# A two-layer decoder trunk on one core: the order of all five engines written out, with the convolution and the second compression in one tiled block

## The chip, the core and the metric

The kernel runs on one core of one Trainium2 chip (trn2). The metric is device time in microseconds (us) of one execution, median over runs; the profile is of one more execution. The engines are TensorE (PE: matmuls, with PEld its weight loads), VectorE (DVE), ScalarE (ACT), GpSimd (POOL) and SyncE (SP, which here only issues loads).

## The reference, cut to what matters

```python
def hybrid_layer(x, ...):                       # x: (1, 256, 1024), two layers
    h = rms_norm(x, norm_g)
    z = h @ w_in                                # 3612 columns, split among three groups of heads
    o_a = fox_attention(q, k, v, f_logit) * silu(f_gate)         # 4 heads x 64, forget gates
    o_b = conformer_conv(glu_in, ...) * silu(c_gate)             # 31 causal taps on 256 channels
    o_c = nsa_attention(q, kc, vc, ks, vs, kw, vw, ...) * silu(n_gate)
    return x + concat(o_a, o_b, o_c) @ w_out
# in nsa_attention (8 query heads in 2 groups g):
def compress(x, pe, w1, w2):                    # blocks of 32 tokens, stride 16: 15 blocks
    blk = x[:, cmp_idx] + pe                    # -> (15 blocks, 2 groups, 32 * 64)
    return gelu(blk @ w1) @ w2                  # w1: 2048 x 256, w2: 256 x 64
k_cmp = rope(compress(kc, pe_k, k_w1, k_w2), cmp_end)
v_cmp = compress(vc, pe_v, v_w1, v_w2)
# branches: softmax over compressed blocks, over selected blocks, over a window; mixed by gates
```

A final norm follows the second layer. All of it is fp32.

## The kernel before

**Products in halves.** An fp32 weight tile comes by DMA in raw form (512 KB for 1024 columns); ACT copies it to a "hi" half (L240), DVE subtracts to get the "lo" half (L244), and PE then makes three products, hi by hi, hi by lo, lo by hi. The input projection's columns are cut in 24 blocks of 128, S0 to S23 (`wS`), each 24 matmuls (`s(i)`, L457 to L459), two blocks to a PSUM tile named after the even one: `ps0` is S0 and S1 (the raw keys and values to compress), `ps8` S8 and S9 (the first half of the queries), `ps10` S10 and S11 (the second half), and so on. Blocks of the output projection are O0 to O7. The matrices w1 of the two compressions are not cut in halves: eight raw tiles of 512 KB a layer, `ww1_i_q` for compression i, quarter q.

**The work around the change, in each layer.** `blocks` (L781) adds the position terms to the raw keys and values and writes `xp0` and `xp1`. `compress(i)` (L791) is 16 matmuls on a quarter of PE's columns each, four to a row of the order (`32x256 x4`), into `ph0` or `ph1`; in the trace each shows as two records. `fox_pv` (L730) is the forgetting attention's product with its values into `ofx`, 8 matmuls on half of PE's columns. `conv` (L546) is the convolution, 64 matmuls on a quarter of the columns into `pcn`, with taps `cw` that `taps` builds on DVE (L535 of the before). `hidden` (L808) brings the sums of the compressions into `hidT`, and `compressed_kv` (L830, L833) makes the compressed keys and values `pkv` from them with `w2`. `query(i)` turns and splits `ps8` or `ps10` into `qs0` and `qs1` (L474 to L477 and L761 on DVE, L760 on ACT); `scores(n)` (L859, L860) are the window's logits `sw0` to `sw7` and need `qs` and the keys `kh`, `klz`. `fpt` and `fs` are the forgetting attention's transposes and logits.

**Order.** SP, PE and POOL run in the order in which the calls are written (`manual_schedule`). DVE and ACT are placed by the scheduler, apart from the first stretch of layer 0; `mark` and `behind` only fix behind which instruction a half may be formed. `pump` issues the loads in the order of `queue` (built from `S_ORDER`), at most `RAW` = 6 raw tiles being held; a load waits until the tile six loads before it was used: a block S by its lo half, a quarter of w1 by its matmuls. `WARM` is the number of matmuls on a constant that run at the start ahead of the transposes of the norm's gain (`g0p`) and behind them (`turn`, L282).

Of the kernel before, what the change touches and what calls it, by code (L numbers as in the profile page):

```python
# [9 lines left out]
F32 = mybir.dt.float32  # L10
# [9 lines left out]
AHEAD = 4  # L20
WARM = 5, 3
LAST = 416
LAG = 1
# [38 lines left out]
W2 = {"w2k": (0, 128), "w2v": (128, 128), "pw": (256, 512)}  # L62
W2_N = 768
# [63 lines left out]
def trunk(ctx, tc, a, out, dbg=None):  # L127
    nc = tc.nc
# [8 lines left out]
    ctx.enter_context(tc.manual_schedule(engines={E.SP, E.PE, E.Pool}))  # L137
# [33 lines left out]
    S_ORDER = (2, 3, 4, 5, 12, 13, 14, 15, 6, 7, 8, 9, 0, 1, 10, 11, "w1", 16, 17, 18, 19, 20, 21, 22, 23)  # L171
    queue = []
    parts = []
    for l in range(L):
# [21 lines left out]
    marks = [{}]  # L196

    def mark():

        at = {}  # L200
        for i in reversed(nc.cur_bb.bb.instructions):
            if i.engine in (E.DVE, E.Activation) and i.engine not in at and i.name not in formed:
                at[i.engine] = i
            if len(at) == 2:
                break
        marks.append(at)

    formed = set()

    def behind(engine, made):  # L210
        at = marks[-LAG].get(engine) if len(marks) >= LAG else None
        with tc.issue_after(at) if at is not None else nullcontext():
            made()
        formed.add(nc.cur_bb.bb.instructions[-1].name)

# [17 lines left out]
    def split_hi():  # L233

        key, n = parts.pop(0)
# [4 lines left out]
        behind(E.Activation, lambda: sc.copy(hi, w))  # L240
        split[key] = hi, lo

        def low():
            behind(E.DVE, lambda: ve.tensor_tensor(lo, w, hi.bitcast(F32), op=ALU.subtract))  # L244
            used(1)
        return low

    def split_next():
        if not parts or parts[0][0] not in raws:
            return False  # L250
        split_hi()()
        return True

    def need(key, ahead=AHEAD):

        while key not in split:
            assert split_next(), key
        n = sum(1 for k in split)
        while n < ahead + 1 and split_next():
            n += 1  # L260
        return split[key]
# [137 lines left out]
    for l in range(L):  # L399
# [17 lines left out]

        def mprod(t, which, n, steps="xt", p=None):
# [18 lines left out]
            if which == "A":  # L437
                sc.copy(vsw[:, t, :], p[:, :256])
                sc.activation(gl[:, t, :], p[:, 256:280], AF.Tanh, scale=0.5)
            else:  # L440
                sc.copy(fv[:, t, :], p[:, :256])
                ve.tensor_tensor(ff[:, t, :], p[:, 256:260], S("fb"), op=ALU.add)


        bank = {}

        def s(i, ahead=AHEAD):

            mark()
            hi, lo = need(("S", i, l), ahead)  # L450
# [11 lines left out]
        def s2(i):  # L462
            return bank.pop(i // 2).rearrange("p (i t) -> p i t", i=2)
# [27 lines left out]
        def gates(i):  # L491
            p = s2(16 + 2 * i)
            u = cp.tile([128, 2, 256], F32, name=nm(f"tg{i}"), tag="tg", bufs=1)
            sc.activation(u, p, AF.Tanh, scale=0.5)
            ve.scalar_tensor_tensor(sgt[0][:, 2 * i:2 * i + 2], u, 1.0, p, op0=ALU.add, op1=ALU.mult)
# [6 lines left out]
        def mix_split(c0, n, cols=slice(0, 256)):  # L502
            m = sgt[0][:, c0:c0 + n, cols]
            h = mixh[:, c0:c0 + n, cols]
            sc.copy(h, m)
            ve.tensor_tensor(mixl[:, c0:c0 + n, cols], m, h.bitcast(F32), op=ALU.subtract)
# [9 lines left out]

        def glu(i):

            p = s2(2 + 2 * i)
            th = cp.tile([128, 512], F32, name=nm(f"th{i}"), tag="tg", bufs=1)[:, 0:256]  # L520
            sc.activation(th, p[:, 1], AF.Tanh, scale=0.5)
            ve.scalar_tensor_tensor(ypad[:, i, 30:286], th, 1.0, p[:, 0], op0=ALU.add, op1=ALU.mult)
# [8 lines left out]
        def taps(i):  # L531
            if i == 0:
                sgt[0] = cp.tile([128, 2, 32, 32], F32, name=nm("cw"), tag="sg", bufs=1)
            cw = sgt[0][:, i]
            behind(E.DVE, lambda: ve.tensor_tensor(  # L535
                cw, C("sh").unsqueeze(1).broadcast_to([128, 32, 32]),
                S("cw")[:, i * 32:(i + 1) * 32].unsqueeze(2).broadcast_to([128, 32, 32]), op=ALU.mult))
            pconv[i] = pconv[i], cw.rearrange("p (g q) c -> p g q c", g=4)

        def conv():  # L540
            p = pscore(nm("pcn"))
            for i in range(2):
                yr, w = pconv[i]
                for q in range(8):
                    for g in range(4):
                        te.matmul(p[g * 32:(g + 1) * 32, i * 256:(i + 1) * 256], w[:, g, q], yr[:, g, 4 * q:4 * q + 256],  # L546
                                  start=q == 0, stop=q == 7)
            sgt[0] = cp.tile([128, 8, 256], F32, name=nm("sg"), tag="sg", bufs=1)
            for i in range(2):
                sc.activation(yc[:, i], p[:, i * 256:(i + 1) * 256], AF.Identity, bias=S("cb")[:, i:i + 1])  # L550
# [4 lines left out]
        def ln_stats():  # L555
            pt = ln["p"] = ppt(nm("lnp"))
            st = cp.tile([128, 2, 6], F32, name=nm("st"), tag="st", bufs=1)
            mv = ln["mv"] = cp.tile([128, 2, 2], F32, name=nm("mv"), tag="mv", bufs=1)
            rv = ln["rv"] = cp.tile([128, 2], F32, name=nm("rv"), tag="rv", bufs=1)
            for t in range(2):  # L560
                for c in range(2):
                    o = t * 256 + c * 128
                    te.transpose(pt[:, o:o + 128], yc[:, c, t * 128:(t + 1) * 128], C("id"))
            for t in range(2):
# [3 lines left out]
            gp.tensor_tensor(rv, rv, mhalf[:, :2], op=ALU.pow)  # L568
            yn = ln["yn"] = cp.tile([128, 2, 256], F32, name=nm("yn"), tag="rr", bufs=2)
# [4 lines left out]
        def ln_swish():  # L574
            yn = ln["yn"]
            pn = ppt(nm("lnq"))
# [4 lines left out]
            yl = cp.tile([128, 2, 256], F32, name=nm("yl"), tag="rr", bufs=2)  # L581
# [5 lines left out]
            ve.scalar_tensor_tensor(yt, yt, 1.0, yl, op0=ALU.add, op1=ALU.mult)  # L587

        def pointwise():
# [7 lines left out]
            return pcv.rearrange("p (i t) -> p i t", i=2)  # L597
# [15 lines left out]
        def forget():  # L613
            ffv = ff.rearrange("p t h -> p (t h)")
            lsr = cp.tile([128, 512], F32R, name=nm("lsr"), tag="ru", bufs=2)
            lsh, lsl = (lsr[:, c:c + 256].rearrange("p (t h i) -> p t h i", t=2, h=4) for c in (0, 256))
            fx["ls"] = lsh, lsl
            ve.scalar_tensor_tensor(fa, ffv, -1.0, ffv, op0=ALU.mult, op1=ALU.max)
            sc.activation(fe, fa, AF.Exp, scale=-1.0)
# [631 lines left out]
```

## Time and profile before

| | us |
|---|---|
| median of 3 runs (316.72 to 316.84) | 316.83 |
| the profiled execution | 316.37 |
| its span | 314.6 |
| PE busy, of the span | 303.7 (97%) |
| DVE busy, of the span | 234.9 (75%) |
| ACT busy, of the span | 186.9 (59%) |

The span runs from the first instruction to the last; 1.77 us of the profiled execution lie outside it. Matmuls are pipelined, so the busy time of one (280 ns for 256 columns) is longer than the distance from one start to the next (about 120 ns); the distance is what counts when PE is full. A row's start is in us from the span's start.

### The profile page before, as it was taken

Reading aid. Unit: us, or ns where it says so; the run is one execution under the profiler, and the core shown is the slowest. Engines: PE = TensorE matmul, PEld = TensorE weight load, DVE = VectorE, ACT = ScalarE, POOL = GpSimd, SP = SyncE. Lnnn points to the kernel's source line nnn. Section 1 sums busy time; section 2 is a strip of 40 time slices with the busy share of each in tenths; the row PEclk is TensorE's granted clock in tenths of the full one; section 3 lists DMA queues with packets and bytes.
Section 4 is the critical chain, followed back from the end, with each engine's and each line's share of the span. In section 5 each row is a group of like instructions: output and inputs, shape, how many; then the busy total and the mean of one; then the engine's idle time right before and its main releaser. Section 6 shows DMA issues by size and latency. Waiting matters only on the chain.

```text
span 314.6 us, 6713 instructions
## 1 busy us (share of the span) xinstructions
PE 303.7 (97%) x2596; PEld 273.8 (87%) x2596; DVE 234.9 (75%) x626; ACT 186.9 (59%) x408; POOL 22.6 (7%) x49
## 2 busy tenths in 40 slices
PE   7999999999999999999999999999999999999991
PEld 5799999995789999888899999999578999988891
DVE  3957689981999998965574778998199989896532
ACT  4757668731595957861545766783259595786110
POOL 2000043000002000000000003400000200000000
PEclk9999999999999999999999999999999999999998
DMA  7797889707927445130461878880792744000101
GB/s 285 256 382 272 277 246 236 290 2 271 409 69 258 133 135 155 46 94 2 166 200 70 292 233 258 219 307 2 285 403 59 260 135 133 0 2 0 63 8 69
DMA packets 16545, 54.93 MB, mean 175 GB/s; under 512 B 2048, under 2 KB 2560, under 8 KB 16512
## 3 DMA queue, kind: packets, MB, share of 16 engines
q1 hardware_dynamic: 15264, 51.29, 46.9%
q0 software_dynamic: 960, 2.92, 4.1%
q8 instruction: 20, 0.33, 0.4%
q10 hardware_dynamic: 288, 0.28, 0.3%
q14 instruction: 13, 0.11, 0.1%
HBM read 52.85 MB, written 1.64 MB: 173 GB/s over the span
## 4 chain that ended last, share of the span: by engine, by line
PE 88%; issue 4%; DMA 4%; DVE 1%; ACT 1%; POOLq 0%; POOL 0%; DVEq 0%
PE ps L457 15%; PE ps L458 14%; PE ps L459 14%; PE pcn L546 4%; PE pA L430 4%; PE pt L915 4%; PE pB L430 4%; PE pw L982 4%; PE pw L979 4%; PE pw L978 4%; PE on L928 3%; DMA ww<-in_w 3%; PE sw L859 2%; PE sw L860 2%; DMA cf<-in_cf 1%
## 5 line engine op out<-in xcount | busy, mean ns | idle before, releaser
L457 PE MATMUL ps<-hTh,wS_1h 128*128 128x256 f32 x192 | 54.3, 283 | 0.0
L457 PE MATMUL ps<-hTh,wS_0h 128*128 128x256 f32 x192 | 54.3, 283 | 0.0
L459 PE MATMUL ps<-hTh,wS_1l 128*128 128x256 f32 x192 | 53.9, 281 | 0.0
L458 PE MATMUL ps<-hTl,wS_0h 128*128 128x256 f32 x192 | 53.9, 281 | 0.0
L459 PE MATMUL ps<-hTh,wS_0l 128*128 128x256 f32 x192 | 53.9, 281 | 0.0
L458 PE MATMUL ps<-hTl,wS_1h 128*128 128x256 f32 x192 | 53.9, 281 | 0.0
L887 ACT ACTIVATE P<-P,mx 128x128 f32<-128x128 f32 (+1 forms) x64 | 28.5, 447 | 15.1 <-DVE mx L482 15.0
L457 PEld LDWEIGHTS ps<-hTh,wS_1h 128*128 128x128 f32 x192 | 36.2, 188 | 0.6 <-issue 0.4
L457 PEld LDWEIGHTS ps<-hTh,wS_0h 128*128 128x128 f32 x192 | 36.2, 188 | 0.6 <-issue 0.4
L458 PEld LDWEIGHTS ps<-hTl,wS_1h 128*128 128x128 f32 x192 | 36.2, 188 | 0.2
L458 PEld LDWEIGHTS ps<-hTl,wS_0h 128*128 128x128 f32 x192 | 36.2, 188 | 0.2
L459 PEld LDWEIGHTS ps<-hTh,wS_1l 128*128 128x128 f32 x192 | 36.2, 188 | 0.0
L459 PEld LDWEIGHTS ps<-hTh,wS_0l 128*128 128x128 f32 x192 | 36.2, 188 | 0.0
L244 DVE TENSOR_TENSOR wS_0l<-wS,wS_0h 128x1024 fp32r<-128x1024 f32 x24 | 28.6, 1221 | 8.4 <-ACT wS_0h L240 8.4
L244 DVE TENSOR_TENSOR wS_1l<-wS,wS_1h 128x1024 fp32r<-128x1024 f32 x24 | 28.5, 1221 | 8.1 <-ACT wS_1h L240 8.1
L240 ACT CAST wS_1h<-wS 128x1024 fp32r<-128x1024 f32 x24 | 24.1, 1051 | 1.8 <-DMA wS<-in_wS 1.8
L240 ACT CAST wS_0h<-wS 128x1024 fp32r<-128x1024 f32 x24 | 24.1, 1049 | 0.5 <-DMA wS<-in_wS 0.4
L482 DVE CUSTOM_DVE_ANT_0 P<-sw,cf 128x128 f32<-128x128 f32 (+1 forms) x64 | 19.5, 355 | 2.4 <-PE sw L860 2.4
L917 ACT COPY PT<-pt 128x512 f32<-128x512 f32 x24 | 13.6, 586 | 9.6 <-PE pt L915 9.6
L985 DVE TENSOR_TENSOR x<-pw,x 128x512 f32<-128x512 f32 (+1 forms) x9 | 5.7, 631 | 16.8 <-PE pw L982 16.8
L485 DVE TENSOR_SCALAR P<-P,co 128x128 f32<-128x128 f32 (+1 forms) x64 | 16.4, 316 | 0.1
L546 PE MATMUL pcn<-yr,cw 128*32 128x256 f32 x256 | 14.2, 380 | 0.0
(239 smaller groups left out, 679.3 us busy)
## 6 DMA issues: line engine op xcount, KB each, us to landing
wS<-in_wS SPq DMA_DIRECT2D x48, 512.0 KB, 5.7
ww<-in_w SPq DMA_DIRECT2D x16, 512.0 KB, 5.3
wO<-in_wo SPq DMA_DIRECT2D x16, 512.0 KB, 4.0
yr<-ybuf POOLq DMA_DIRECT2D x16, 142.0 KB, 5.0
wA<-in_wA SPq DMA_DIRECT2D x4, 420.0 KB, 4.2
wB<-in_wB SPq DMA_DIRECT2D x4, 390.0 KB, 5.0
x<-in_x SPq DMA_DIRECT2D x2, 512.0 KB, 4.1
w<-in_w SPq DMA_DIRECT2D x2, 384.0 KB, 4.7
```

The costliest lines, as they stand in the source:

```text
L240: behind(E.Activation, lambda: sc.copy(hi, w))
L244: behind(E.DVE, lambda: ve.tensor_tensor(lo, w, hi.bitcast(F32), op=ALU.subtract))
L430: te.matmul(p[:, :n], a_[:, k, tok], b_, start=first, stop=s_ == "t" and k == 7)
L457: te.matmul(o, hi[:, k], hTh[:, k], start=k == 0, stop=False)
L458: te.matmul(o, hi[:, k], hTl[:, k], start=False, stop=False)
L459: te.matmul(o, lo[:, k], hTh[:, k], start=False, stop=k == 7)
L482: ve.tensor_tensor_reduce(o, x, m, -1.0, 3.0e38, ALU.add, ALU.min, mx)
L485: ve.tensor_scalar(x, x, r, None, op0=ALU.mult)
L546: te.matmul(p[g * 32:(g + 1) * 32, i * 256:(i + 1) * 256], w[:, g, q], yr[:, g, 4 * q:4 * q + 256], start=q == 0, stop=q == 7)
L887: sc.activation(P[:, g, b], P[:, g, b], AF.Exp, bias=mx[:, c:c + 1], scale=-1.0, accum_out=su[:, c:c + 1])
L915: te.transpose(pt[:, o + b * 128:o + (b + 1) * 128], Pg[:, b * 128:(b + 1) * 128], C("id"))
L917: sc.copy(PT, pt)
```

## The change

All five engines now run in written order: `E.DVE` and `E.Activation` join `manual_schedule`, `mark`, `behind`, `need` and `AHEAD` are gone, and the helpers are cut in steps (`form_hi` and `form_lo`, `mask` and `expo`, `query_rope` and `query`, `gate_tanh` and `gate_mul`, ...) that a long list of calls puts in order. Every formation of a half stands at a place of its own. The number of instructions is the same but for the rows below.

```diff
-WARM = 5, 3
+WARM = 8, 1
-    ctx.enter_context(tc.manual_schedule(engines={E.SP, E.PE, E.Pool}))
+    ctx.enter_context(tc.manual_schedule(engines={E.SP, E.PE, E.Pool, E.DVE, E.Activation}))
-    S_ORDER = (2, 3, 4, 5, 12, 13, 14, 15, 6, 7, 8, 9, 0, 1, 10, 11, "w1", 16, 17, 18, 19, 20, 21, 22, 23)
+    S_ORDER = (2, 3, 4, 5, 12, 13, 14, 15, 6, 7, 0, 1, 8, 9, "w1a", 10, 11, "w1b", 16, 17, 18, 19, 20, 21, 22, 23)
...
-            for g in range(2):
-                for m in range(2):
-                    te.matmul(pk[g * 64:(g + 1) * 64, 0:16], w2k[:, m], gk[:, m, g * 16:(g + 1) * 16],
-                              start=m == 0, stop=m == 1)
+                te.matmul(pk[:, 0:32], w2k[:, m], gk[:, m], start=m == 0, stop=m == 1)
+            for m in range(2):
...
+            kcp = cp.tile([128, 16], F32, name=nm("kcp"), tag="kcp", bufs=1)
+            for g, (r, r2) in enumerate(halves):
+                sc.copy(kcp[r], pk[r, g * 16:(g + 1) * 16])
...
+        fox_pv()
+        query_rope(0)
+        compress(0)
+        query(0, 0)
+        query(0, 1)
+        taps(0)
+        taps(1)
+        s(10)
+        part(0)
+        scores(0)
+        scores(1)
+        s(11)
...
+        conv(0)
...
+        conv(1)
...
+        compress(1)
```

So one `turn` matmul more stands in front of the start in all (nine for eight); S0 and S1 run before S8 and S9; w1 is loaded in two pieces; the first product of `compressed_kv` is 2 matmuls on all columns where it was 4 on half (its `w2` is 896 columns wide where it was 768, and is loaded behind S23 where it stood between two quarters of w1), with two small ACT copies more.

On PE, before, this stands where the forgetting attention's product ends (`ofx`), in layer 0; `ph0` stands right ahead of these rows, and the last three are the first of S11:

```order
L730 MATMUL ofx_0_1022<-fPT11_0_922,fv_0_129 64x256
L730 MATMUL ofx_0_1022<-fPT10_0_916,fv_0_129 64x128
L730 MATMUL ofx_0_1022<-fPT11_0_922,fv_0_129 64x128
L791 MATMUL ph1_0_1031<-ww1_1_0_0_691,xp1_0_964 32x256 x4
L791 MATMUL ph1_0_1031<-ww1_1_1_0_722,xp1_0_964 32x256 x4
L791 MATMUL ph1_0_1031<-ww1_1_2_0_1000,xp1_0_964 32x256 x4
L791 MATMUL ph1_0_1031<-ww1_1_3_0_1006,xp1_0_964 32x256 x4
L457 MATMUL ps10_0_970<-hTh_114,wS_11_0h_718 128x256
L458 MATMUL ps10_0_970<-hTl_115,wS_11_0h_718 128x256
L459 MATMUL ps10_0_970<-hTh_114,wS_11_0l_719 128x256
```

On PE now, at the first of two places, `ofx` ends, and `ph0` and the first of S10 follow:

```order
L735 MATMUL ofx_0_949<-fPT11_0_933,fv_0_130 64x128
L803 MATMUL ph0_0_966<-ww1_0_0_0_636,xp0_0_881 32x256 x4
L803 MATMUL ph0_0_966<-ww1_0_1_0_642,xp0_0_881 32x256 x4
L803 MATMUL ph0_0_966<-ww1_0_2_0_674,xp0_0_881 32x256 x4
L803 MATMUL ph0_0_966<-ww1_0_3_0_715,xp0_0_881 32x256 x4
L431 MATMUL ps10_0_998<-hTh_115,wS_10_0h_887 128x256
L432 MATMUL ps10_0_998<-hTl_116,wS_10_0h_887 128x256
```

Here `ph1` no longer follows `ofx`. The second place on PE, after S10, the first two `sw` and S11:

```order
L524 MATMUL pcn_0_1085<-yr0_0_453,cw_0_995 32x256 x32
L524 MATMUL pcn_0_1085<-yr1_0_530,cw_0_995 32x256 x32
L803 MATMUL ph1_0_1182<-ww1_1_0_0_891,xp1_0_937 32x256 x4
L803 MATMUL ph1_0_1182<-ww1_1_1_0_947,xp1_0_937 32x256 x4
L803 MATMUL ph1_0_1182<-ww1_1_2_0_971,xp1_0_937 32x256 x4
L803 MATMUL ph1_0_1182<-ww1_1_3_0_977,xp1_0_937 32x256 x4
L942 MATMUL pt00_0_1216<-cf_68,P0_0_1059 128x128 x4
L882 MATMUL sw2_0_1221<-kh0_0_893,qs0_0_958 128x256
```

`ph1` went from between `ofx` and S11 to behind the convolution, past S10, S11 and the first two `sw`; `ofx` and `ph0` changed places, and S10, which stood ahead of `ph0`, stands behind it.

On DVE, before, the first half of the queries in layer 0 (`q0r`, `q0u`, then `qs`), and the position terms (`xp`) behind it:

```order
L475 TENSOR_TENSOR q0u_0_878<-ps8_0_780,cf_68 128x512
L710 RECIPROCAL fsu1_0_814<-fsu1_0_814 128x4
L476 TENSOR_TENSOR q0r_0_877<-q0r_0_877,cf_68 128x512
L485 TENSOR_SCALAR fP1_0_812<-fP1_0_812,fsu1_0_814 128x128
L485 TENSOR_SCALAR fP1_0_812<-fP1_0_812,fsu1_0_814 128x256
L485 TENSOR_SCALAR fP1_0_812<-fP1_0_812,fsu1_0_814 128x128
L485 TENSOR_SCALAR fP1_0_812<-fP1_0_812,fsu1_0_814 128x256
L477 TENSOR_TENSOR q0u_0_878<-q0u_0_878,q0r_0_877 128x512
L761 SCALAR_TENSOR_TENSOR qs0_0_875<-q0u_0_878,qs0_0_875 64x512
L761 SCALAR_TENSOR_TENSOR qs1_0_876<-q0u_0_878,qs1_0_876 64x512
L781 TENSOR_TENSOR xp0_0_958<-ps0_0_887,sm_0_88 64x16x15 x4
L781 TENSOR_TENSOR xp1_0_964<-ps0_0_887,sm_0_88 64x16x15 x4
```

On DVE now, the same work, among lo halves of S10 and S11 and the split of the keys (`klz`):

```order
L793 TENSOR_TENSOR xp0_0_881<-ps0_0_751,sm_0_88 64x16x15 x4
L230 TENSOR_TENSOR wS_10_0l_888<-wS_10_0_728,wS_10_0h_887 128x1024
L755 TENSOR_TENSOR klz0_119<-ku_0_781,kh0_0_893 64x512
L755 TENSOR_TENSOR klz1_120<-ku_0_781,kh1_0_894 64x512
L793 TENSOR_TENSOR xp1_0_937<-ps0_0_751,sm_0_88 64x16x15 x4
L230 TENSOR_TENSOR wS_11_0l_944<-wS_11_0_837,wS_11_0h_943 128x1024
L448 STREAM_SHUFFLE q0r_0_960<-ps8_0_854 128x512
L449 TENSOR_TENSOR q0u_0_961<-ps8_0_854,cf_68 128x512
L450 TENSOR_TENSOR q0r_0_960<-q0r_0_960,cf_68 128x512
L451 TENSOR_TENSOR q0u_0_961<-q0u_0_961,q0r_0_960 128x512
L771 SCALAR_TENSOR_TENSOR qs0_0_958<-q0u_0_961,qs0_0_958 64x512
L771 SCALAR_TENSOR_TENSOR qs1_0_959<-q0u_0_961,qs1_0_959 64x512
```

The position terms went ahead of the queries, and the queries behind the lo half of S11; the taps follow them at once, where they stood some 50 rows earlier.

On SP, before, the loads of the second compression's quarters in layer 0:

```order
L225 DMA ww1_0_2_0_648<-in_w1 128x1024
L225 DMA ww1_0_3_0_654<-in_w1 128x1024
L225 DMA ww1_1_0_0_691<-in_w1 128x1024
L225 DMA ww1_1_1_0_722<-in_w1 128x1024
L770 DMA w2_0_956<-in_w2 128x768
L225 DMA ww1_1_2_0_1000<-in_w1 128x1024
L225 DMA ww1_1_3_0_1006<-in_w1 128x1024
L225 DMA wS_16_0_1012<-in_wS 128x1024
```

On SP now, from the first compression's quarters on:

```order
L203 DMA ww1_0_2_0_674<-in_w1 128x1024
L203 DMA ww1_0_3_0_715<-in_w1 128x1024
L203 DMA wS_10_0_728<-in_wS 128x1024
L203 DMA wS_11_0_837<-in_wS 128x1024
L203 DMA ww1_1_0_0_891<-in_w1 128x1024
L203 DMA ww1_1_1_0_947<-in_w1 128x1024
L203 DMA ww1_1_2_0_971<-in_w1 128x1024
L203 DMA ww1_1_3_0_977<-in_w1 128x1024
L203 DMA wS_16_0_983<-in_wS 128x1024
L203 DMA wS_17_0_989<-in_wS 128x1024
```

Two blocks S stand between the two compressions' quarters, and the load of `w2` is gone from among them.

## Rows read from the trace of the kernel before

**Rows 1.** Page, part 1: busy us, share of the span, instructions

```profile
PE 303.7 (97%) x2596; PEld 273.8 (87%) x2596; DVE 234.9 (75%) x626; ACT 186.9 (59%) x408; POOL 22.6 (7%) x49
```

**Rows 2.** Page, part 2: clock granted to PE, 40 slices, in tenths

```profile
PEclk9999999999999999999999999999999999999998
```

**Rows 3.** Waits of PE: what for, us in total, times, longest

```profile
PE ph L791 <- DMA ww<-in_w: 1.3, 2, 0.6
```

**Rows 4.** Chain that ended last, both layers: start us, us, what

```profile
72.36 4.38 DMA ww<-in_w
...
82.29 7.04 PE pcn L546 x128
...
221.48 4.41 DMA ww<-in_w
...
225.93 0.64 PE ph L791 x8
```

**Rows 5.** Timeline of PE, 71 to 81 us: start, us, instructions, [idle before]

```profile
71.23 1.93 PE L791 MATMUL ph<-ww,xp 128*32 128x256 f32 x32
73.09 1.52 PE L730 MATMUL ofx<-fPT,fv 128*64 128x256 f32 x16
74.55 1.59 PE L791 MATMUL ph<-ww,xp 128*32 128x256 f32 x24
76.78 0.64 PE L791 MATMUL ph<-ww,xp 128*32 128x256 f32 x8 [0.65 <-DMA ww<-in_w]
77.35 0.39 PE L457 MATMUL ps<-hTh,wS_0h 128*128 128x256 f32 x1
...
80.29 0.97 PE L808 MATMUL hidT<-cf,part 128*128 128x32 f32 x8
```

**Rows 6.** Timeline of SP, which issues the loads, from 71.9 us

```profile
71.93 0.80 SPq L225 DMA_DIRECT2D ww<-in_w  x2
```

**Rows 7.** Timeline of ACT, 66 to 80 us

```profile
66.16 1.29 ACT L760 ACTIVATE qs<-q0u 64x512 fp32r<-64x512 f32 x2
...
78.05 1.05 ACT L240 CAST wS_0h<-wS 128x1024 fp32r<-128x1024 f32 x1 [0.19 <-DMA wS<-in_wS]
79.33 1.06 ACT L240 CAST wS_0h<-wS 128x1024 fp32r<-128x1024 f32 x1 [0.23 <-DMA wS<-in_wS]
```

**Rows 8.** Timeline of DVE, 62 to 80 us

```profile
62.08 0.75 DVE L474 STREAM_SHUFFLE q0r<-ps 128x512 f32<-128x512 f32 x1
...
65.05 0.68 DVE L477 TENSOR_TENSOR q0u<-q0u,q0r 128x512 f32<-128x512 f32 x1
66.83 1.39 DVE L761 SCALAR_TENSOR_TENSOR qs<-q0u,qs 64x512 fp32r<-64x512 f32 x2 [1.09 <-ACT qs L760]
68.57 3.36 DVE L781 TENSOR_TENSOR xp<-ps,sm 64x240 f32<-64x240 f32 x8 [0.36 <-PE ps L459]
79.13 1.23 DVE L244 TENSOR_TENSOR wS_0l<-wS,wS_0h 128x1024 fp32r<-128x1024 f32 x1 [7.20 <-ACT wS_0h L240]
```

**Rows 9.** Windows: busy us (count) of each engine, granted clock, DMA share, GB/s

```profile
74.00:86.00 12.00, 11.35 (x152) 8.07 (x152) 6.71 (x25) 4.48 (x14) 0.00 (x0) 1.00 1.02 410
```

**Rows 10.** Timeline of all engines, the first 12 us

```profile
0.92 2.50 PE L282 MATMUL turn<-idle 128*128 128x512 f32 x5 [0.92 <-DVE idle L275]
...
4.69 1.97 PE L288 MATMUL g0p<-cf 128*128 128x128 f32 x8 [1.27 <-DMA cf<-in_cf]
...
6.22 1.41 DVE L338 SCALAR_TENSOR_TENSOR h<-x,rs,g0p 128x512 f32<-128x512 f32 x2 [0.67 <-POOL rs L332]
...
6.32 1.62 PE L282 MATMUL turn<-idle 128*128 128x512 f32 x3
6.84 0.89 ACT L240 CAST wA_0h<-wA 128x840 fp32r<-128x840 f32 x1 [0.39 <-DMA wA<-in_wA]
...
7.74 1.07 PE L354 MATMUL hp<-cf,h 128*128 128x128 f32 x8
...
9.02 0.69 DVE L360 TENSOR_TENSOR hTl<-hp,hTh 128x512 fp32r<-128x512 f32 x1 [0.47 <-ACT hTh L356]
```

More of the change, by code (lines that the diff above doesn't have):

```diff
@@ L239, in split_hi, with form_lo @@
         lo = wp.tile([128, 1024], F32R, name=nm + "l", tag="lo", bufs=HILO)[:, :n]
-        behind(E.Activation, lambda: sc.copy(hi, w))
+        sc.copy(hi, w)
         split[key] = hi, lo
-        def low():
-            behind(E.DVE, lambda: ve.tensor_tensor(lo, w, hi.bitcast(F32), op=ALU.subtract))
-            used(1)
[L246 to L261, printed above, removed]
+        lows.append((lo, w, hi))
+    def form_lo():
+        if lows:
+            lo, w, hi = lows.pop(0)
+            ve.tensor_tensor(lo, w, hi.bitcast(F32), op=ALU.subtract)
+            used(1)
     load_x(0)
@@ L1022, in trunk, with proj0, nx_scale, proj1 @@
-        mark()
-        need(("S", 2, l), 7)
-        mprod(1, "B", NB)
-        s(2)
+        TA, TB = slice(0, 128), slice(128, 256)
+        pj = {}
+        nxt = Norm(l + 1)
+        last = l + 1 == L
+        def proj0(n, ks):
+            if n not in pj:
+                pj[n] = pz(nm(f"pw0{n}"))
+            project(0, n, pj[n], ks)
+        def nx_scale():
+            h = nxt.scale(0)
+            if last:
+                store(0, h)
+        def proj1(ks):
+            if "b" not in pj:
+                pj["b"] = pz(nm("pw10"))
+            project(1, 0, pj["b"], ks)
+            if 7 in ks:
+                for i in range(4):
+                    del split["O", i, l]
@@ new lines, in proj2, with res1 @@
+        def proj2(i):
+            if last:
+                p = pj["c", i] = pz(nm(f"pw1{i}"))
+                project(1, 1, p, range(8), i * 256, 256)
+            else:
+                if i == 0:
+                    pj["c"] = pz(nm("pw11"))
+                project(1, 1, pj["c"], range(4 * i, 4 * i + 4))
+                for k in (4 + 2 * i, 5 + 2 * i):
+                    del split["O", k, l]
+        def res1():
+            residual(1, 0, 512, pj["b"])
+            if last:
+                last_norm(1, slice(0, 512), nxt)
@@ new lines, in trunk @@
+        form_hi()
+        form_lo()
+        bias_heads()
+        s(6)
+        form_lo()
+        fox_k()
+        fox_k0()
+        fox_kl()
+        s(7)
+        form_hi()
+        form_lo()
+        form_hi()
+        fox_scores(0)
+        form_lo()
+        fox_scores(1)
+        fox_scores(2)
+        fox_mask(0)
+        fox_exp(0)
+        s(0)
+        fox_mask(1)
+        fox_exp(1)
+        keys_rope()
+        form_hi()
+        fox_scores(3)
+        fox_norm(0)
+        s(1)
+        fox_mask(2)
@@ new lines, in trunk @@
+        fox_mask(3)
+        fox_exp(2)
+        fox_exp(3)
+        form_lo()
+        fox_trans(0, 0)
+        fox_norm(1)
+        fox_trans(0, 1)
+        fox_copy(0, 0)
+        s(8)
+        fox_copy(0, 1)
+        blocks(0)
+        form_hi()
+        form_lo()
+        keys_hi()
+        fox_trans(1, 0)
+        fox_trans(1, 1)
+        keys_lo(0)
+        s(9)
+        fox_copy(1, 0)
+        fox_copy(1, 1)
+        keys_lo(1)
+        blocks(1)
+        form_hi()
+        form_lo()
+        fox_pv()
@@ new lines, in trunk @@
+        norms(1, 0)
+        norms(1, 1)
+        trans(0, 0)
+        trans(0, 1)
+        scores(2)
+        part(1)
+        hidden()
+        ptcopy(0)
+        load_w2()
+        s(16)
+        form_hi()
+        hidden_in()
+        form_lo()
+        gelu()
+        ln_trans()
+        s(17)
+        form_hi()
+        ln_stats()
+        mask(2, 0)
+        form_lo()
+        expo(2, 0)
+        form_hi()
+        ln_norm()
+        trans(1, 0)
+        trans(1, 1)
+        scores(3)
+        gate_tanh(0)
@@ new lines, in trunk @@
+        s(20)
+        swish()
+        ptcopy(2)
+        form_hi()
+        expo(3, 0)
+        form_lo()
+        expo(3, 1)
+        cmp_scores(0)
+        coeff(3)
+        gate_tanh(1)
+        scores(4, (1,))
+        norms(3, 0)
+        cmp_soft(0)
+        s(21)
+        norms(3, 1)
+        gate_mul(1)
+        form_hi()
+        form_lo()
+        pointwise()
+        mask(4, 0)
+        gate_tanh(2)
+        cmp_norm(0)
+        expo(4, 0)
+        trans(3, 0)
+        gate_mul(2)
```

774 lines of the change are left out of this document (443 added, 331 removed).

## Prediction

> **What bounds the kernel now.** The first thing to read is the page. PE is busy for 97% of the span, DVE for 75%, ACT for 59% [rows 1], and PE's granted clock reads full in every slice up to the last [rows 2]. So PE's stream of matmuls is the time, and a change can only pay where that stream has a gap or an avoidable step. The second view is the list of PE's waits: its other entries lie where a layer begins, and between those stands one, `ph` for a load of w1, 1.3 us in two times, once a layer [rows 3]. The third is the chain: it leaves PE for that load, for 4.38 us in layer 0 and 4.41 us in layer 1 [rows 4]. Those 8.8 us are the time from issue to landing, during which PE had other work; they are not what the wait costs.
>
> What it costs is seen in PE's timeline [rows 5]. `ph0` runs from 71.23 to 73.09, 1.86 us; `ofx` follows to 74.55; `ph1`, the same 32 records, runs from 74.55 to 77.35, 2.80 us, with 0.65 us of recorded idle. The convolution has matmuls of the same shape, and its 128 records take 7.04 us [rows 4], 55 ns each; 32 of them would take 1.76 us. `ph1` is therefore 1.04 us dearer than its work.
>
> The load is late because SP issues the last two quarters at 71.93 [rows 6], when the first quarters of `ph0` have given their tiles back, and `ph1` wants them 2.6 us later. Behind them the next tiles come one after the other: the first two copies of ACT, for S16 and S17, start at 78.05 and 79.33, each after a wait for its load [rows 7], so a 512 KB tile takes 1.28 us in a full burst. DVE meanwhile waits 7.20 us for the first of these halves [rows 8]. In the 12 us from 74 on the DMA engines are full (share 1.02, 410 GB/s) while DVE works 6.71 and ACT 4.48 us [rows 9]. DVE's pause costs nothing by itself, since PE has work.
>
> The start is its own stage [rows 10]: five `turn`s, `g0p`, three `turn`s, then the first transposes `hp` at 7.74, although the first half of their input `h` is done at about 6.92 (half of DVE's 1.41 us from 6.22).
>
> **The change, part by part.** *The second compression goes behind the convolution.* In the frame of the old times, S9 now ends where S10 began: 71.23 less a block of 2.94 us (S11's 77.35 to 80.29 [rows 5]), 68.3. `ofx` (1.46) and `ph0` (1.86) end at 71.6. The last two quarters are issued as `ph0` gives tiles back, by about 71; at 4.4 us plus one tile of 1.28 they land by 76.7. `ph1` comes after S10, S11, eight `sw` (about 1 us) and 7.04 us of convolution: 71.6 + 5.9 + 1.0 + 7.0 = 85.5, 9 us later than the load. It also follows matmuls of its own shape. I take 1.76 us for it: 1.04 us saved a layer, **-2.08 us** in two. If it costs what `ph0` costs, the saving is 0.94 a layer; if only the recorded idle goes, 0.65. Bounds: -1.3 to -2.1.
>
> *The queries now stand between S9 and `sw0`.* `sw0` starts 1.46 + 1.86 + 2.94 = 6.26 us after S9's end, at 74.6. From S9's end DVE needs four steps of about 0.7 us (62.08 to 65.73 with other work between them), ACT half of its 1.29, and DVE 0.69 twice [rows 7, 8]: 2.8 + 0.65 + 1.4, about 5.0 with hand-overs, so 73.3. That leaves 1.2 us if DVE is free when S9 ends. Ahead of it in DVE's fixed order stand, since S1, the eight `xp` (3.36), two splits of keys (1.4), two lo halves (2.46) and the scales of one pair of heads (about 1.2, an estimate from rows on 128 partitions of similar length): 8.4 us. PE gives them two blocks (5.9) and 12 transposes (1.6, by `hp`'s eight in 1.07): 7.5. DVE may thus be 0.9 us late, and 0.3 us of margin is left. I take no stall, with a bound of 0.5 us a layer. If the cover is gone, what waits is `sw0`, and with it all of PE. The taps (two steps of about 1.2 us) come behind the queries; the convolution is at 78.5 and they end at about 76, so 2.5 us to spare.
>
> *Lo halves at fixed places.* The halves of S6 now stand behind the forgetting attention's bias rows, and `s(6)` wants them at once. The price lies between nothing and one lo half, 1.23 us [rows 8]; the formation overlaps with the first products, which need only the hi half, so I take the low end, 0.1 us a layer, **+0.2 us**.
>
> *The load of `w2` behind S23.* S19 and S21 to S23 are issued as `ph1` frees tiles, from 86 on, and `w2` behind them: 86 + 4.4 + five tiles of 1.28 gives 96.8. `pkv` comes after S16, S17, S18 (8.8), and the transposes and `sw` between them (about 3): 87.3 + 11.8 = 99. Cost nothing, with 2 us of cover. The changed product of `pkv`, and ACT's two small copies a layer, touch no queue that is waited for there: nothing, within 0.1 us either way.
>
> *One `turn` behind `g0p`.* With one instead of three (1.62 us in all) PE is free when the first half of `h` is there, so the first four `hp` can start near 6.95. ACT is held until 7.73 by its first weight copy (6.84 + 0.89), so `hTh` moves from 8.4 to about 7.75. Behind it `hTl` had waited 0.47 us for ACT; that is all DVE can give back. PE's first products wait for `hTl`, hence **-0.45 us**. Bounds: none, if the weights' loads turn out to pace this stage, to -0.65.
>
> The sum goes against the profiled execution, 316.37 us (its span of 314.6 and 1.77 outside it): -2.08 - 0.45 + 0.2 = -2.33, so 314.04. The median of the runs, 316.83, stands 0.46 above that execution; I carry it over: **314.5 us**.
>
> One level matters at the start. `g0p`'s eight transposes take 1.97 us and `hp`'s eight of the same shape 1.07 [rows 10]: the first run at half the clock, the second at full. The new order has eight `turn`s at once (to about 4.4) and less filler later; a pause of up to about 0.5 us may stand ahead of `hp`. The row of the old start has a pause of 1.27 us ahead of `g0p`, and the clock came up all the same. [...] The rows show no fall after a pause of such a length, so I go by them.
>
> **The rivals.** *The start gives nothing or loses.* If `hp`'s eight run at half clock, they cost 0.9 us more; the term turns from -0.45 into +0.45: 315.4. If it is only void: 315.0.
>
> *The loads are late.* The first compression's quarters and S10, S11 are now issued between blocks in use, and `w2` at the end of a burst. If a tile takes 1.8 instead of 1.28 us there, `w2` is 2.6 us later and `pkv` waits about 0.6; twice, with a little at S19, that is 1 to 1.5 us: 315.5 to 316. For it speaks the full share in the burst [rows 9], against it the cover of 2 us.
>
> *DVE's fixed order becomes the bound (slower than before).* With a scheduler gone, one late step holds everything behind it on DVE: `sw0` waits for the queries, the convolution for the taps, and the masks behind them. The margin is the 0.3 us above. The gain of 2.33 is eaten if the queries are 1.5 us a layer later than I reckon; at 2.5 us it costs 4.4: 318.9, and 318 halfway. For it: DVE has 8.4 us of work in a stretch of 7.5. Against: half of that work was there before in the same stretch without a wait of PE's.
>
> *The change doesn't do what it says*, since the quarters are still late: this would need the load to take 9 us longer; I give it nothing.
>
> **How the numbers follow.** The forecast 0.54 (its own range 313.6 to 315.0), the start void or losing 0.14, late loads 0.10, a partial stall of DVE that eats most of the gain 0.08 (316.2 to 317), DVE as the bound 0.14. A change of 0.2% is 0.63 us, about what a measurement here can tell; faster means below 316.2. The first three cases are faster, 0.78; the fourth is the same, 0.08; the last slower, 0.14. The range is 313.3 to 316.9: below it lies a twentieth (a better start), above it the last case.
>
> **What the profile will show.** Right: no row of `ph` waiting for `ww`; `ph` in the second place at 55 ns a record; `hTh` before 8 us; PE without a wait between 13 and 308 us. Wrong: a row of `sw`, `pcn` or `ps` waiting for DVE or ACT, above all at the queries and at S6; `pkv` waiting for `w2`; `hp`'s eight near 2 us. Any wait of more than 1.2 us a layer in those places would make the forecast wrong.

## The result, and the profile after

The changed kernel takes 314.44 us (median of 6 runs, 313.85 to 315.07); the kernel before, in the same comparison, 316.85 (316.72 to 318.56). The ratio is 0.9902, with an interval of 0.9877 to 0.9928. The forecast was 314.5. A second comparison of the same two gave 314.62 against 317.57, ratio 0.9906 (0.9879 to 0.9933): the time of the changed kernel repeats, that of the kernel before moves more, and why it does is part of what follows. One execution of the kernel before and three of experiment 3, which lie well above the others of their kernel, count in none of the ratios.

The profiled execution took 314.83 us, with a span of 313.0; that is 1.6 us less span than before. First the row of the page that answers to [rows 1]:

```profile
PE 302.5 (97%) x2589; PEld 274.4 (88%) x2589; DVE 240.9 (77%) x626; ACT 187.5 (60%) x412; POOL 20.9 (7%) x49
```

PE is still 97% of the span; it is the same kind of kernel. Next PE's waits (answers to [rows 3]; columns as there):

```profile
PE pA L402 <- ACT hTh L326: 0.8, 2, 0.5
PE hp L324 <- DVE h L308: 0.7, 1, 0.7
PE pkv L848 <- DVE wS_1l L230: 0.4, 1, 0.4
PE pkv L848 <- DMA w<-in_w: 0.4, 1, 0.4
PE ps L433 <- DVE wS_0l L230: 0.2, 1, 0.2
```

No row of `ph` waits for `ww`. In its place stand `pkv` (once in each layer, 0.4 us; the name behind the arrow is the last event before the wait ended) and `ps`, a block S that waits for its low half. The chain shows the moved pieces (answers to [rows 4, 5]; start us, us, what):

```profile
68.35 1.45 PE ofx L735 x16
69.80 1.86 PE ph L803 x32
...
78.45 7.04 PE pcn L524 x128
85.50 1.73 PE ph L803 x32
...
89.32 9.98 DMA w<-in_w
```

The chain counts the second `ph` from the modelled end of the convolution, 1.73 us. From its first start to the start of what follows it takes 1.84 us (85.31 to 87.15), where it took 2.80 with its wait, counted the same way. The last row is the load of `w2`: it now lies on the chain, and lands at 99.3.

A ledger of PE's timeline puts both profiles side by side. Each entry is the start of a group of matmuls; the third column is the difference of the two before it, the last how it changed since the entry above. `pA` are the first products with the weights `wA` (their second run is called the dense run below), `lnq` and `pw` are matmuls behind S19 and at the end of a layer.

| start of (us) | before | after | after - before | change |
|---|---|---|---|---|
| layer 0: second run of `pA` | 12.70 | 12.52 | -0.18 | |
| S13 | 38.14 | 38.09 | -0.05 | +0.13 |
| first `fs` (S13, S14, S15, S6, S7 lie before) | 52.34 | 52.74 | +0.40 | +0.45 |
| S16 (the changed middle lies before) | 90.34 | 88.93 | -1.41 | -1.81 |
| `lnq` (S16 to S19 and `pkv` lie before) | 104.03 | 103.26 | -0.77 | +0.64 |
| layer 1: S13 | 187.25 | 186.53 | -0.72 | +0.05 |
| first `fs` | 201.45 | 201.14 | -0.31 | +0.41 |
| S16 | 239.51 | 237.23 | -2.28 | -1.97 |
| `lnq` | 253.20 | 251.59 | -1.61 | +0.67 |
| last products `pw` | 296.29 | 294.67 | -1.62 | -0.01 |

So the middle of a layer gained 1.8 to 2.0 us, where the forecast had 1.04; two other stages lost 0.41 to 0.45 and 0.64 to 0.67 a layer, where it had 0.1 and nothing. In the two profiled executions the gain is 1.6 us, where the forecast's sum had 2.33. That the median came within 0.1 us of the forecast is luck: errors of opposite signs nearly cancel.

**The middle.** Of the 1.81 us, the two `ph` give 0.96 (4.67 us together before, 3.71 now). The convolution gives 0.11, 6.93 us for 7.04; this belongs to the placement, since it is 6.93 wherever `ph` follows it (experiment 1 too) and 7.04 wherever the transposes `pt` do (experiment 2 too). The placement is thus worth 1.07 a layer. The first `sw`s give 0.28, and the forgetting attention's transposes 0.46, and these were in no term. PE's timeline before shows one set of six and the block behind it:

```profile
60.78 1.03 PE L719 MATMUL fpt<-cf,fP 128*128 128x128 f32 x6
61.57 0.36 PE L457 MATMUL ps<-hTh,wS_0h 128*128 128x256 f32 x1
```

and DVE's timeline before shows the scaling of what they transpose:

```profile
60.33 0.99 DVE L485 TENSOR_SCALAR fP<-fP,fsu 128x128 f32<-128x128 f32 x4
```

The transposes start at 60.78 while the four scalings run until 61.32: PE takes each piece as DVE hands it over, and six transposes take 0.79 us. Now, on PE and on DVE:

```profile
61.17 0.82 PE L723 MATMUL fpt<-cf,fP 128*128 128x128 f32 x6
61.75 0.37 PE L431 MATMUL ps<-hTh,wS_0h 128*128 128x256 f32 x1
```

```profile
57.65 1.01 DVE L459 TENSOR_SCALAR fP<-fP,fsu 128x128 f32<-128x128 f32 x4
```

The scaling now ends at 58.66, 2.5 us before the transposes start, and the six take 0.58. The list of waits holds no row for this in either kernel: a matmul's modelled end reaches past the start of the next, and holds of less than 0.1 us apiece (starts 0.11 to 0.19 us apart before, 0.11 now) vanish under it. They are to be read from the distance of starts.

The experiments below separate the two causes. With the placement alone (experiment 1) a set of six still takes 0.79 us; with the written order and without the placement (experiment 2) it takes 0.57.

**S6.** Before the low halves that S6 and the next blocks need, DVE does the last step of the bias rows:

```profile
45.45 0.48 DVE L648 SCALAR_TENSOR_TENSOR cLR<-cc,cf,ct 128x256 fp32r<-128x256 f32 x1
45.96 3.50 DVE L230 TENSOR_TENSOR wS_0l<-wS,wS_0h 128x1024 fp32r<-128x1024 f32 x3
```

The first of the three low halves, S6's, starts behind the last bias row and ends at about 47.2. PE's weight loads, at the third product of S6, the first that needs the low half:

```profile
47.24 0.19 PEld L433 LDWEIGHTS ps<-hTh,wS_0l 128*128 128x128 f32 x1 [0.42 <-DVE wS_0l L230]
```

**`pkv`.** SP's loads, and PE at the end of S18:

```profile
86.31 2.98 SPq L203 DMA_DIRECT2D wS<-in_wS  x6
89.32 0.45 SPq L779 DMA_DIRECT2D w<-in_w  x1
```

```profile
98.77 0.28 PE L433 MATMUL ps<-hTh,wS_0l 128*128 128x256 f32 x1
99.44 0.60 PE L848 MATMUL pkv<-gk,w 128*128 128x32 f32 x4 [0.39 <-DMA w<-in_w]
```

Six blocks S are issued from 86.31 on, then `w2`, which takes 9.98 us to land at 99.30; S18's last matmul starts at 98.77. In layer 1:

```profile
237.69 0.44 SPq L779 DMA_DIRECT2D w<-in_w  x1
```

```profile
247.78 0.60 PE L848 MATMUL pkv<-gk,w 128*128 128x32 f32 x4 [0.43 <-DVE wS_1l L230]
```

The row names a low half on DVE, which ended at 247.72. But `w2` landed at 247.64, and in experiment 6 `pkv` starts at 246.57 while that same half runs until 247.08: `pkv` doesn't need the half, and in both layers the wait is for `w2`.

### The profile page after: what moved, and what is told of

Its sections match the earlier page's. It is cut to its first block, busy times and chain, and to the rows that moved or that the text cites. A ratio compares the mean times of both kernels' runs of the same rounds, so it can differ in the third digit from the quotient of the medians.

```text
span 313.0 us, 6703 instructions
## 1 busy us (share of the span) xinstructions
PE 302.5 (97%) x2589; PEld 274.4 (88%) x2589; DVE 240.9 (77%) x626; ACT 187.5 (60%) x412; POOL 20.9 (7%) x49
## 4 chain that ended last, share of the span: by engine, by line
PE 66%; DVE 14%; ACT 6%; DMA 6%; issue 6%; SPq 0%; POOLq 0%; POOL 0%; DVEq 0%
PE ps L433 9%; PE ps L431 9%; PE ps L432 9%; PE pA L402 4%; PE pB L402 4%; PE pw L1018 4%; PE pw L1021 4%; PE pw L1017 4%; PE pt L942 3%; DMA w<-in_w 3%; PE on L962 3%; DVE wS_1l L230 3%; PE pcn L524 2%; DMA wA<-in_wA 2%; ACT wS_1h L222 2%
## 5 line engine op out<-in xcount | busy, mean ns | idle before, releaser
L942 PE MATMUL pt<-cf,P 128*128 128x128 f32 x96 | 13.7, 277 | 0.0
```

The lines of the kernel that those rows point to most:

```text
L942: te.transpose(pts[n][:, o + b * 128:o + (b + 1) * 128], Pg[:, b * 128:(b + 1) * 128], C("id"))
```

## The experiments

Each time stands against the kernel before on the same chip: 317.46 us (median) for the first four, 317.57 for the next four, 317.79 for the two after these. A ratio is taken to that kernel's executions, with its 95% interval.

**1. The moved compression alone, in the kernel before.** DVE and ACT stay with the scheduler.

```diff
         fox_pv()
-        compress(1)
         s(11, 1)
         query(1)
-        hidden()
-        gelu()
...
         conv()
+        compress(1)
...
             if n == 0:
+                hidden()
+                gelu()
                 s(16)
```

> The kernel before, with one part of the change: the second compression's matmuls go behind the convolution, the hidden sums behind the third window scores. DVE and ACT stay with the scheduler. Theory A (the terms of the prediction): the placement is nearly the whole gain, 1.04 us a layer, so 2.1 us less than before, about 314.7, and no row of ph waiting for a load. Theory B (what the stages of the two traces show): the placement gives 1.0 us a layer too, but the middle of a layer became 1.8 us shorter in the changed kernel, and the other 0.85 us a layer, in the transposes fpt and the scores sw, belong to DVE's written order; so fpt still takes 0.8 us and sw0 and sw1 1.1 us here. Rival C: the loads of S18 to S23 become late instead and nothing is gained, 316.8 or more.

Measured: 316.19 us, ratio 0.9966 (0.9952 to 0.9979), about 1.1 us less. The two `ph` together take 3.71 us a layer, exactly as in the changed kernel: 0.96 us a layer, with the convolution's 0.11 1.07, is the placement's. But PE's waits have two rows that the kernel before lacks (`cs` are the logits against the compressed keys),

```profile
PE cs L939 <- ACT P L887: 1.0, 2, 0.5
PE sw L859 <- DVE qs L761: 0.9, 2, 0.6
```

and its timeline shows the second of them behind the moved block:

```profile
86.20 1.91 PE L791 MATMUL ph<-ww,xp 128*32 128x256 f32 x32
...
89.58 0.39 PE L859 MATMUL sw<-kh,qs 128*128 128x256 f32 x1 [0.64 <-DVE qs L761]
```

The third window scores came earlier and met the second half of the queries, which DVE finished at 89.5. By the medians about half of the 2.1 us was given back; in the profiled execution, the slowest of the twelve, more than that, since the rows of `cs` cost it as well. So theory A, that the placement is nearly the whole gain, fails as a statement on the time, though its size for `ph` is right; B's 0.8 us for the transposes is met (0.79), and its 1.1 us for the first scores nearly (1.04).

**2. The compression back, in the changed kernel.** S10 and S11 are loaded ahead of the quarters of w1.

```diff
-    S_ORDER = (..., 8, 9, "w1a", 10, 11, "w1b", 16, ...)
+    S_ORDER = (..., 8, 9, 10, 11, "w1a", "w1b", 16, ...)
...
+        compress(0)
         fox_pv()
         query_rope(0)
-        compress(0)
+        compress(1)
```

> The changed kernel with the second compression back where it was (first compression, forgetting attention's product, second compression), and S10, S11 loaded ahead of all quarters of w1 as before; the rest as changed. Theories A and B: ph waits for w1 again, the second ph costs 2.8 us for 1.8, 1.0 us a layer, so about 2 us more than the changed kernel, 316.4. Against: if PE had other slack there, the time stays near 314.4.

Measured: 318.76 us, ratio 1.0048 (1.0027 to 1.0069): about 4.5 us more than the changed kernel, twice what both theories said. PE's timeline at the second compression:

```profile
72.30 0.64 PE L803 MATMUL ph<-ww,xp 128*32 128x256 f32 x8 [0.49 <-DMA ww<-in_w]
73.56 0.64 PE L803 MATMUL ph<-ww,xp 128*32 128x256 f32 x8 [0.63 <-DMA ww<-in_w]
74.85 0.64 PE L803 MATMUL ph<-ww,xp 128*32 128x256 f32 x8 [0.65 <-DMA ww<-in_w]
```

Three of its four quarters come late, at the 1.28 us of the burst, and the second `ph` takes 4.25 us in layer 0 and 4.06 in layer 1, where the theories had 2.8. In the kernel before, whose scheduler formed halves early, the second quarter went out at 57.50, right behind S11's low half. Here it goes out at 68.56 and the last two right behind it, as the first compression's matmuls and S11's half (done at 68.7) give their tiles back: a low half formed just in time also gives its raw tile back just in time. Besides, S10 stands ahead of the first compression in the kernel before and behind the second here, so PE comes to the second compression at 71.17 instead of 74.55. Which of the two costs how much, no run separates. The written order and the moved compression belong together; the one without the other costs more than the sum suggests.

**3. DVE and ACT back with the scheduler, in the changed kernel.**

```diff
-    ctx.enter_context(tc.manual_schedule(engines={E.SP, E.PE, E.Pool, E.DVE, E.Activation}))
+    ctx.enter_context(tc.manual_schedule(engines={E.SP, E.PE, E.Pool}))
```

> The changed kernel with DVE and ACT given back to the scheduler (all calls and loads as changed, only these two engines' order is free). Theory A: the written order of DVE and ACT is worth nothing by itself, so about 314.4. Theory B: the fpt transposes and the scores fall back by up to 0.85 us a layer, while the low half of S6 may be formed as soon as it can (0.4 us a layer back), so 315 to 316. Rival: without the hints that held formations back, halves are formed far too early or late and DVE's order is much worse, 318 or more.

Measured: 326.82 us, the median of three executions (323.71 to 327.70), ratio 1.0272 (1.0222 to 1.0321). PE's longest waits, in a profiled execution that took 330.4 us:

```profile
PE hidT L823 <- ACT part L811: 3.9, 2, 2.1
PE ps L431 <- DVE fq L663: 3.6, 1, 3.6
```

The rival came true: even the fastest execution is above 318. In the profiled one PE's mean granted clock was 0.969, where it was 0.997 in the fastest (323.71 us), so its length can't be put down to the waits alone. The experiment tells that the free order without hints is far worse, not how much the written order gains over the old hints; for that there is only experiment 1, whose ratio of 0.9966 against 0.9902 leaves 2.0 us to the rest of the change.

**4. The warm-up alone, in the kernel before.**

```diff
-WARM = 5, 3
+WARM = 8, 1
```

> The kernel before with only the warm-up changed: eight matmuls on the constant ahead of the gain's transposes and one behind, where it was five and three. Theory A: 0.45 us less, 316.4, with the first copy of the transposed input at 7.75 instead of 8.40. Theory B: the first weight copy of ACT waits for its load, which lands between 6.8 and 7.4 us from one run to the next, so the gain is 0 to 0.45. Rival: the clock falls back and the first transposes take 2 us for 1.1, 0.5 us more than before.

Measured: 317.17 us, ratio 0.9994 (0.9978 to 1.0009), no difference that can be told. The timeline of its start:

```profile
7.06 1.31 PE L354 MATMUL hp<-cf,h 128*128 128x128 f32 x8
...
7.75 1.25 ACT L356 CAST hTh<-hp 128x512 fp32r<-128x512 f32 x2
```

`hTh` starts at 7.75, as theory A had it, and the second run of `pA` at 12.18 for 12.70: the mechanism is there, 0.5 us in this execution, and its size is below what the times of the kernel before allow to see. The eight `hp` take 1.31 us, so the rival's 2 us isn't there.

**5 to 8. The two new waits, one at a time and together, in the changed kernel.** Experiment 5 is the changed kernel itself.

> The changed kernel once more, as the measure for the next three on the same chip: 0.9902 of the kernel before within the two intervals, and the same three places of loss in the profile (S6 for its low half, pkv for w2, a start that differs from one execution to the next).

Measured: 314.62 us (314.04 to 315.32). Experiment 6 issues the load of `w2` earlier:

```diff
         s(11)
+        load_w2()
...
         ptcopy(0)
-        load_w2()
```

> The changed kernel with the load of w2 issued right behind S11's matmuls, ahead of the loads of S18 to S23. Theory B (the wait of pkv is the load of w2, 10 us from issue to landing behind six tiles): the last S18 matmul and pkv lie close together, 0.55 us a layer less, 1.1 us less than the changed kernel. Theory A (the load had 2 us of cover; the wait has another cause, the low half of S19 or the gates that feed pkv): no change. Rival: w2 pushes S18 to S23 back by a tile and a block S waits for its half instead.

Measured: 313.29 us (312.97 to 313.55), ratio 0.9867 (0.9844 to 0.9891); 1.3 us less than experiment 5. `w2` lands at 81.6, and `pkv` follows S18 without a gap:

```profile
98.83 0.28 PE L433 MATMUL ps<-hTh,wS_0l 128*128 128x256 f32 x1
98.95 0.53 PE L848 MATMUL pkv<-gk,w 128*128 128x32 f32 x4
```

Theory A falls. Experiment 7 forms S6's halves ahead of the bias rows:

```diff
         fox_q()
+        form_hi()
+        form_lo()
         bias_rows()
-        form_hi()
         s(15)
         form_hi()
-        form_lo()
         form_hi()
         form_lo()
```

> The changed kernel with the two halves of S6 formed between the split of the queries and the bias rows, ahead of them on ACT and DVE, and the halves of S7 and S0 behind. Theory B: S6's third matmul no longer waits, 0.4 us a layer, 0.8 us less than the changed kernel. Theory A (0.1 us a layer): 0.2 us less. Rival: the bias rows become late instead and the first forgetting scores wait for them or for the keys, no gain.

Measured: 314.65 us (313.48 to 315.13), no change of the median. Its profiled execution (313.48 us, the fastest of the six) has no wait at S6 in either layer, 0.4 us each, and no late bias rows, but the first scores take 1.08 and 1.10 us for 0.95, and `pkv` waits 0.5 us in layer 1. Where the slower executions lose the gain of S6, no profile shows; the load of `w2`, which is still late, is the likely place. Alone the edit is worth nothing that can be told, as its rival had it, though not for the rival's reason. Experiment 8 is both:

> Both edits together. Theory B: the two waits are in different stages and add up, 1.9 us less than the changed kernel, with no wait of PE left between 13 us and the end. Theory A: 0.2 us less. Rival: the earlier finish of one stage only brings the next late load or half forward, and less than the sum is left.

Measured: 312.82 us (312.57 to 313.53), ratio 0.9855 (0.9831 to 0.9879); 1.8 us less than experiment 5, against 1.9 expected. With `w2` early, the halves of S6 are thus worth about 0.5 us in the medians of experiments 6 and 8. They are not free: the first scores take 1.05 and 1.10 us here for 0.95, since PE comes to them earlier and DVE ends the queries no sooner (at 74.1 us for 73.9). This is a version that beats both kernels. PE's waits, apart from the very first `turn`, are these two, at the start and, for `pA` once, where layer 1 begins:

```profile
PE hp L324 <- DVE h L308: 0.9, 1, 0.9
PE pA L402 <- ACT hTh L326: 0.5, 2, 0.3
```

**9 and 10. The start.** Experiment 9 is the kernel of 8 again.

> The kernel with w2 and S6 early once more, as the measure for the next one on the same chip: 0.985 to 0.986 of the kernel before; PE's first dense stretch (the second run of pA) begins 5.1 us after the first weight tile wA lands, 12.2 to 12.6 us.

Measured: 312.97 us, ratio 0.9856; the second run of `pA` at 12.52, 5.1 us after `wA` landed at 7.41. Experiment 10 loads the first weight tile ahead of the second half of x:

```diff
     load_x(0)
+    later = queue[1:]
+    del queue[1:]
+    pump()
+    queue.extend(later)
     load_x(1)
...
             cur.squares(0)
-            cur.squares(1, "s-")
             cur.rms(0)
             cur.scale(0)
             form_hi()
+            cur.squares(1, "s-")
```

> The same with the first weight tile loaded ahead of the second half of x, and ACT's first weight copy ahead of the squares of that half. Theory S (in the changed kernel the landing of wA paces the start): wA lands by about 6, the first copy of the transposed input no longer waits for it, and the dense stretch begins 0.2 to 0.5 us earlier, near 12.1, in every execution. Rival: the second half of x becomes the late one, its squares and so the second norm slip by as much, and nothing or a loss is left.

Measured: 312.72 us, ratio 0.985 (0.9825 to 0.9875). The timeline of its start:

```profile
5.71 0.89 ACT L222 CAST wA_0h<-wA 128x840 fp32r<-128x840 f32 x1 [0.29 <-DMA wA<-in_wA]
...
7.20 1.31 PE L328 MATMUL hp<-cf,h 128*128 128x128 f32 x8 [1.01 <-DVE h L312]
...
8.07 1.07 ACT L330 CAST hTh<-hp 128x512 fp32r<-128x512 f32 x2
```

The weight copy starts at 5.71 and holds nothing up any more. `hTh` starts at 8.07, and the second run of `pA` at 12.34: now the squares of the late half of x stand ahead of `hTh` on ACT. 0.2 us in the profile and in the medians, which is within what these times can tell; theory S is right in kind, and the rival took part of it back.

**11 and 12. The kernel before, twice more, for its profile.** Each is one execution.

> The kernel before once more, for its profile: its times in the runs so far go from 316.3 to 319, and the profiled one was 316.37. Theory: the slower executions lose at the start, where the clock comes up only behind the first transposes hp (eight in 1.9 us for 1.1) or the first loads land 0.3 us later, and the dense stretch begins near 13.6 for 12.7; the middle of the layers is the same. Rival: they lose in the middle, where sw waits for the queries on DVE or ph waits longer for w1.

> The same once more, to see whether the place of the loss is the same in a second execution.

The first took 317.06 us, the second 318.14. In the second the start is, from the timeline,

```profile
4.81 1.97 PE L288 MATMUL g0p<-cf 128*128 128x128 f32 x8 [1.39 <-DMA cf<-in_cf]
...
7.86 1.92 PE L354 MATMUL hp<-cf,h 128*128 128x128 f32 x8
...
8.96 0.58 ACT L356 CAST hTh<-hp 128x512 fp32r<-128x512 f32 x1 [1.10 <-PE hp L354]
```

with the eight `hp` at 1.92 us for 1.07 in [rows 10], and the second run of `pA` at 13.44 for 12.70. Of PE's waits in it:

```profile
PE sw L859 <- DVE qs L761: 0.9, 2, 0.7
```

Both the theory and its rival are met in it: 0.7 us at the start, and 0.9 us at `sw` for the queries on DVE. The first has the eight `hp` at 1.11 us, the dense run at 12.98, and 0.3 us at `sw`.

## Why the prediction was right, by its own steps

**The second compression (-2.08).** Right: 1.07 us a layer for 1.04, shown in the changed kernel and, alone, in experiment 1. The step took 1.76 us for `ph` behind matmuls of its own shape; `ph` takes 1.84 and the convolution ahead of it 0.11 less. No profile with this order of PE has a row of `ph` that waits.

**The queries.** Right, with a little more margin than reckoned. DVE's timeline (answers to [rows 8]):

```profile
67.92 1.23 DVE L230 TENSOR_TENSOR wS_0l<-wS,wS_0h 128x1024 fp32r<-128x1024 f32 x1
...
69.18 0.74 DVE L448 STREAM_SHUFFLE q0r<-ps 128x512 f32<-128x512 f32 x1
...
72.50 1.41 DVE L771 SCALAR_TENSOR_TENSOR qs<-q0u,qs 64x512 fp32r<-64x512 f32 x2 [0.70 <-ACT qs L770]
```

S9 ended at 68.3, DVE was held by S11's low half until 69.1, 0.8 us late as reckoned (0.9), and the queries were done at 73.9. `sw` starts at 74.5: a margin of 0.6 for 0.3. What the step left out is the other side of the written order. In the kernel before DVE hands PE the scaled logits with no margin at all, and the second half of the queries so late that the third `sw` waits 0.3 to 0.9 us in some executions (experiments 11, 12 and 4); neither profile of the changed kernel has such a row. The assumption that failed is that PE's list of waits is complete: the sum had no term for holds that the list does not resolve, 0.46 us a layer at the transposes alone.

**S6 (+0.2).** The place was right, the term mis-sized: +0.41 to +0.45 a layer, for 0.1. The low half starts only when the two splits of the forgetting attention's queries and the five steps of the bias rows are through, and PE reaches its third product before it ends. The prediction took the low end of its range, nothing to 1.23, on the ground that the half overlaps with the first products; it does, but only two products, about 0.2 us, come before the first that needs it.

**`w2` (nothing).** Wrong: its stage lost 0.64 to 0.67 us a layer, about 0.5 of it as a hold in front of `pkv`, shown by experiment 6, which got 1.3 us back. The cover of 2 us was reckoned with five tiles ahead of `w2` from 86 on, at 1.28 us each; there were six, and between the landing of the first, 89.71, and of the last, 98.18, lie five steps of 1.7 us on average, among them two of 2.8 and 2.0. The rival of late loads had this as its case, with 1.8 us a tile and 0.6 a layer (by its own terms, 96.8 + 2.6 against 99, it should have said 0.4). So this rival came true together with the forecast, and what it costs was paid by the gain of the middle that no term had. `ps` at S6 and `pkv` for `w2` were also named as signs of being wrong; together they cost 1.1 us a layer, just under the 1.2 that the prediction allowed.

**The start (-0.45).** Right when the weights land early: with `WARM` at 8, 1 and `wA` landing at 6.8 to 6.9 the dense run begins at 12.13 (experiment 2) and 12.18 (experiment 4), 0.5 us before 12.70. In the profile after `wA` landed at 7.41, and 0.18 us was left. From the timeline of the start (answers to [rows 10]):

```profile
0.93 3.78 PE L252 MATMUL turn<-idle 128*128 128x512 f32 x8 [0.93 <-DVE idle L245]
...
4.73 1.33 PE L258 MATMUL g0p<-cf 128*128 128x128 f32 x8
...
7.01 1.31 PE L324 MATMUL hp<-cf,h 128*128 128x128 f32 x8 [0.74 <-DVE h L308]
7.43 0.89 ACT L222 CAST wA_0h<-wA 128x840 fp32r<-128x840 f32 x1 [0.93 <-DMA wA<-in_wA]
...
8.23 1.07 ACT L326 CAST hTh<-hp 128x512 fp32r<-128x512 f32 x2
```

ACT's copy of `wA` waits for its load, and `hTh` stands behind it. Over the executions with the changed order, landings of 7.02, 7.17, 7.41, 7.48 and 7.90 gave the dense run at 12.13, 12.28, 12.52, 12.59 and 13.01: 5.11 us behind the landing each time; a landing at 6.80 (experiment 2) gave 12.13 too, so below 7 us something else holds the start. The bound "if the weights' loads turn out to pace this stage" was the relevant one.

**The carry of 0.46 us.** The median of before was taken as 0.46 above its profiled execution. That execution happened to hold few of its small losses; another lost 1.8 us more of span, at the start and around `sw` (experiment 12). Neither loss stands in the two profiles of the changed kernel, whose eight `hp` take 1.31 us, their two halves lying apart, and whose `sw` do not wait. Its own profiled execution lies 0.4 us above its median, that of the kernel before 0.5 below; this is why the paired medians differ by 2.4 to 3.0 us and the two spans by 1.6.

In the end, in the spans: placement -2.1, the rest of the middle -1.6, S6 +0.9, `w2` +1.3, and next to nothing left of the start by S13: -1.6. The forecast had -2.1, nothing, +0.2, nothing and -0.45.

## What to carry to other kernels

When one engine is 97% busy, read its gaps from the distance of starts and not from the list of waits; small holds by a supplier without margin are a term of their own (0.46 us a layer here), and here they are part of what made one execution of the kernel before differ from the next. A step that is moved away from a late load should be followed to the next load in the same queue: here the seventh transfer of a burst arrived 10 us after its issue, and issuing this small tile, which is needed once, ahead of the burst gave 1.3 us. Forming operands just in time frees an engine's order, but holds their raw tiles longer, and so delays the loads behind them: 11 us for one quarter of w1 in experiment 2.

## What the runs showed of the hardware that was not expected

How fast PE did its first real work differed with the matmuls at the start, and, with the old start, from one execution to the next. The distance of starts shows two rates: in the first profile of the kernel before, the eight `g0p` start 0.21 us apart, and the eight `hp`, of the same shape, 0.11 us apart, in both behind the first two. The prediction called this half the clock and the full one; the granted clock reads 1.00 over the first 12 us in that profile, and in the changed kernel's too, so the rate is read from the starts alone.

With five matmuls on a constant, a recorded pause of 1.3 to 1.6 us, `g0p` and three more, the eight `hp` took 1.07 and 1.11 us in two profiles (the first and experiment 11), and 1.92 us in two others (experiments 1 and 12). With eight at once and one behind, `g0p` followed with a recorded pause of 0.2 us in experiment 10 and none in the others. In eight of ten profiles it took 1.09 to 1.49 us where it took 1.97 before; in the changed kernel, at 1.33, its starts go from 0.21 to 0.11 us apart behind the fourth. In the other two (experiments 4 and 7) it took 1.97 and 1.95. `hp` took 1.31 or 1.32 us in all ten, its two halves lying apart, although a pause of 0.6 to 1.2 us stands recorded ahead of it in eight of them. The prediction had priced a rival of +0.45 us on `hp` at the slower rate. That rate is found for `hp` at the old start, whose five matmuls end 1.3 us and more before `g0p`, and not at the new one. No run varies the first run of matmuls and the filler behind `g0p` one at a time, so which of the two counts isn't shown.

The first weight tile landed between 6.8 and 7.9 us after the span's start in the 13 profiles with the same loads ahead of it. In the changed kernel alone it was 7.41 and 7.90.
